# The opening of a two-layer decoder step written in a fixed order: first weights split behind the third turned block, high products ahead of block 4, rstd rows spread in one go

## The chip, the cores and the metric

The kernel runs on one core of a Trainium2 chip. A core has five engines that each work through a queue of their own in order: TensorE (PE in the profile; PEld are its weight loads), VectorE (DVE), ScalarE (ACT), GpSimd (POOL) and SyncE (SP, which here only issues DMA transfers). They wait for one another on semaphores. The metric is the time of one execution in microseconds (us), the median of several runs.

## What is computed

One step of a two-layer trunk, for 512 prompt tokens and 64 sample tokens (8 sequences of 8), model width 1024, all in 32-bit floats. Layer 0 begins with an RMSNorm and one input projection into 2560 columns, which the change is about; causal gating, differential attention over the prompt and over 64 pages of cached keys and values, an output projection and a SwiGLU follow, then a layer with a diagonal state-space scan and another SwiGLU.

```python
def rmsnorm(x, g):
    xf = x.astype(jnp.float32)
    y = xf * lax.rsqrt(jnp.mean(xf * xf, axis=-1, keepdims=True) + EPS)
    return (y * g.astype(jnp.float32)).astype(x.dtype)

def even_project(h, w_in, sgu_norm):      # h = rmsnorm(x, norm_mix[0])
    b, t, _ = h.shape
    p = h @ w_in
    uv = jax.nn.gelu(p[..., :2 * A_WIDTH])
    u = uv[..., :A_WIDTH]
    v = rmsnorm(uv[..., A_WIDTH:], sgu_norm)
    ...
    return u, v, q, k, vb
```

## The kernel before

The 576 tokens lie along the free dimension and the model width along the partitions, in 8 blocks of 128 (`k` from 0 to 7). x arrives token by token in rows, so each block is first turned by TensorE: four transposes of 128 x 128 into a PSUM tile `xT`, and a short one of the 64 sample tokens into `xU` (lines 430 to 450). x is loaded in two halves of columns, `load_x(0)` for blocks 0 to 3 and `load_x(1)` for blocks 4 to 7, five tiles `xt` each, with the first weights between them.

Every product of two f32 matrices is made of three at the faster rate of rounded operands: each operand is split into a high part (`gxh`, `wh`, rounded by a copy on ACT) and a low part (`gxl`, `wl`, the difference), and high x high, low x high and high x low are summed in PSUM. So a turned block is used three times: ACT scales it by the norm's weight into `gxh`, DVE makes `gxl`, and DVE copies the unscaled block to `x`, which SP stores to `dX` for the residual. Meanwhile the squares of x are summed along the width (`square`, on ACT with an accumulator, and two of the ten on POOL with a reduction on DVE).

The weights come in pairs of column blocks, 1 MB a load (`raw`, two buffers). A unit is one block of 128 output columns: `wsplit` makes `wh` and `wl` (two buffers each), and `unit_mm` runs 8 blocks x 3 products x 2 halves of 288 tokens, 48 matmuls. Ten pairs make twenty units. The first unit takes the blocks in order as they come (`kmajor`): for each block, the three products of the one half and then of the other. Its weight split is issued behind block 3 (`KSPL`), with the low part on POOL (`GLO`), that of the second unit on DVE.

The norm's factor per token, rstd, is applied late: `ev_scaled` multiplies a finished unit by `rb`, rstd spread over all partitions. `Stat0.steps` makes rstd out of the sums by a chain of small DVE operations (`rstd_from`, three Newton steps), and `bcast_rows` spreads it by five small matmuls into two PSUM tiles `rbp` and `rbq`; behind the second of them ACT may already copy the first 256 columns.

PSUM has eight banks: four for products (`mbank`, which also takes every second `xT`), four for all else (`bank`). SBUF blocks come from a ring of 44.

What sets the order: this is written in a language whose scheduler places each instruction on its engine's queue by its own forecast, apart from instructions wrapped in `keep`, which stay in program order, and stretches under `tc.manual_schedule()`, which are issued as written. The opening before uses `keep` for the turns; products, squares on POOL, weight splits and the DMAs of SP are placed by the scheduler. Behind the opening, side jobs (`tables`, which loads small constants, the mixer's weights `sgw` and the page table `ptt`; then `sample_attn`, which gathers pages `pg` through `pidx`, made of `ptt`, and turns each key page, `ktp`) are stepped in between units by `drv`.

## Time and profile before

| | us |
|---|---|
| runs shown (3) | 1392.58, 1394.92, 1396.45; median 1394.92 |
| the profiled execution | 1402.85 |
| its span, first to last instruction | 1401.1 |
| PE busy in the span | 1364.9 (97%) |
| DVE, ACT, POOL busy | 844.3, 484.8, 263.7 |
| first product (`acc`) of the projection | starts at 17.87 |
| third unit | starts at 36.05 |
| first page turned (`ktp`) | starts at 54.22 |

All later times are from the profiled execution, counted from the start of its span. A row of the timeline gives the start, the time until the instruction's end, the engine, the line, the operation, what it writes and reads, shapes, and how many alike were merged; in brackets stands how long the engine had been idle and who released it. Ends overlap the next start where work is pipelined, so the spacing of starts tells the rate. Engines other than the one that ends last may idle at no cost.

### The profile page before, as it was taken

Reading aid. Unit: us, or ns where it says so; the run is one execution under the profiler, and the core shown is the slowest. Engines: PE = TensorE matmul, PEld = TensorE weight load, DVE = VectorE, ACT = ScalarE, POOL = GpSimd, SP = SyncE. Lnnn points to the kernel's source line nnn. Section 1 sums busy time; section 2 is a strip of 40 time slices with the busy share of each in tenths; the row PEclk is TensorE's granted clock in tenths of the full one; section 3 lists DMA queues with packets and bytes.
Section 4 is the critical chain, followed back from the end, with each engine's and each line's share of the span. In section 5 each row is a group of like instructions: output and inputs, shape, how many; then the busy total and the mean of one; then the engine's idle time right before and its main releaser. Section 6 shows DMA issues by size and latency. Waiting matters only on the chain.

```text
span 1401.1 us, 27629 instructions
## 1 busy us (share of the span) xinstructions
PE 1364.9 (97%) x11382; PEld 1304.8 (93%) x11382; DVE 844.3 (60%) x1985; ACT 484.8 (35%) x875; POOL 263.7 (19%) x387
## 2 busy tenths in 40 slices
PE   8999999999999999999999989999999999999997
PEld 6888888879999999999999989999999999999997
DVE  5544667578699536887974697444343434443455
ACT  4234664434332223333322556233221221222234
POOL 2453543660000100444461000000000000000002
PEclk9999999999999999999999999999999999999999
DMA  8565544763333432554566791232323223313321
GB/s 248 167 202 178 173 146 127 220 192 93 89 87 114 121 91 73 161 154 135 142 191 216 205 284 57 68 91 61 91 69 111 63 75 106 89 56 98 91 61 69
DMA packets 192726, 177.38 MB, mean 127 GB/s; under 512 B 19420, under 2 KB 168280, under 8 KB 192600
## 3 DMA queue, kind: packets, MB, share of 16 engines
q1 hardware_dynamic: 172168, 118.18, 28.5%
q0 software_dynamic: 18912, 54.42, 13.3%
q10 hardware_dynamic: 1520, 3.02, 0.6%
q8 instruction: 90, 1.47, 0.4%
q14 instruction: 36, 0.29, 0.1%
HBM read 154.24 MB, written 25.53 MB: 128 GB/s over the span
## 4 chain that ended last, share of the span: by engine, by line
PE 84%; DVE 9%; DMA 2%; issue 2%; ACT 2%; SPq 1%; POOL 0%; ACTq 0%; POOLq 0%; DVEq 0%
PE acc L293 71%; PE ktp L808 2%; PE so L875 1%; PE ssc L789 1%; DVE wl L263 1%; PE S L652 1%; PE yp L1729 1%; PE yp L1723 1%; DMA xt<-in_x_sample_dram 1%; DVE x L1066 1%; PE O L685 1%; PE gT L1463 1%; PE satp L849 1%; PE vp L1666 0%; PE AT L677 0%
## 5 line engine op out<-in xcount | busy, mean ns | idle before, releaser
L293 PE MATMUL acc<-hi,wh 128*128 128x288 f32 x2400 | 713.6, 297 | 1.2 <-ACT hi L227 1.2
L293 PE MATMUL acc<-lo,wh 128*128 128x288 f32 x2400 | 707.3, 295 | 0.8 <-DVE lo L228 0.8
L293 PE MATMUL acc<-hi,wl 128*128 128x288 f32 x2400 | 707.5, 295 | 0.4 <-DVE wl L263 0.4
L293 PEld LDWEIGHTS acc<-hi,wh 128*128 128x128 f32 x2400 | 450.2, 188 | 8.3 <-issue 6.2
L293 PEld LDWEIGHTS acc<-lo,wh 128*128 128x128 f32 x2400 | 450.4, 188 | 1.3 <-DVE lo L228 1.3
L293 PEld LDWEIGHTS acc<-hi,wl 128*128 128x128 f32 x2400 | 450.5, 188 | 0.6 <-DVE wl L263 0.6
L260 ACT CAST wh<-raw 128x1024 fp32r<-128x1024 f32 (+2 forms) x194 | 182.8, 944 | 582.6 <-PE acc L293 416.3
L263 DVE TENSOR_TENSOR wl<-raw,wh 128x1024 fp32r<-128x1024 f32 (+2 forms) x193 | 211.7, 1097 | 58.5 <-ACT wh L260 56.7
L1139 DVE TENSOR_TENSOR tu<-acc,rb 128x288 f32<-128x288 f32 x88 | 40.3, 458 | 126.3 <-PE acc L293 126.0
L1876 POOL TENSOR_TENSOR sq<-sq,sq 128x288 f32<-128x288 f32 x12 | 9.6, 801 | 533.4 <-ACT sq L1872 533.4
L293 PE MATMUL acc<-gxh,wh 128*128 128x288 f32 x320 | 99.6, 314 | 0.9 <-DVE proj L390 0.9
L293 PE MATMUL acc<-gxh,wl 128*128 128x288 f32 x320 | 95.5, 301 | 0.6 <-DVE wl L263 0.6
L293 PE MATMUL acc<-gxl,wh 128*128 128x288 f32 x320 | 95.7, 300 | 0.0
L1129 DVE TENSOR_TENSOR tg<-acc,rb 128x288 f32<-128x288 f32 x88 | 39.9, 456 | 90.0 <-PE acc L293 89.0
L1149 DVE TENSOR_TENSOR x<-acc,x 128x288 f32<-128x288 f32 x96 | 43.3, 455 | 70.6 <-PE acc L293 70.5
L751 POOL DMA_INDIRECT pg<-in_cache_k_dram,pidx x64 | 65.5, 1023 | 84.1 <-PE ktp L808 48.8
L751 POOL DMA_INDIRECT pg<-in_cache_v_dram,pidx x64 | 66.0, 1031 | 63.8 <-PE so L875 37.8
L293 PEld LDWEIGHTS acc<-gxh,wh 128*128 128x128 f32 x320 | 60.8, 191 | 6.7 <-issue 6.0
L293 PEld LDWEIGHTS acc<-gxh,wl 128*128 128x128 f32 x320 | 60.7, 190 | 2.2 <-issue 1.1
L293 PEld LDWEIGHTS acc<-gxl,wh 128*128 128x128 f32 x320 | 61.1, 191 | 0.3 <-issue 0.2
L1516 POOL DMA_DIRECT2D dF<-Fn x32 | 20.0, 629 | 130.0 <-DVE Fn L1437 130.0
L227 ACT CAST hi<-tu 128x576 fp32r<-128x576 f32 x44 | 29.7, 676 | 35.0 <-DVE tu L1141 35.0
(464 smaller groups left out, 1601.2 us busy)
## 6 DMA issues: line engine op xcount, KB each, us to landing
raw<-in_w_ffn_in_dram SPq DMA_DIRECT2D x88, 512.0 KB
raw<-in_w_ffn_out_dram SPq DMA_DIRECT2D x24, 768.0 KB
raw<-in_w_in_even_dram SPq DMA_DIRECT2D x10, 1024.0 KB
raw<-in_w_glu_dram SPq DMA_DIRECT2D x16, 512.0 KB
raw<-in_w_out_even_dram SPq DMA_DIRECT2D x8, 512.0 KB
dF<-Fn POOLq DMA_DIRECT2D x32, 128.0 KB
dG<-gt POOLq DMA_DIRECT2D x16, 256.0 KB
dL<-dZ POOLq DMA_DIRECT2D x64, 64.0 KB
```

The costliest lines, as they stand in the source:

```text
L227: A.copy(hi, src)
L260: c = A.copy(hi[:, 0:nk], src)
L263: c = (lo_eng or V).tensor_tensor(lo[:, 0:nk], src, f32(hi[:, 0:nk]), op=ALU.subtract)
L293: PE.matmul(pts[hf], lhsT=w[:, k, :], rhs=x[:, c0:c1], start=(k == 0 and wi == 0), stop=(k == nk - 1 and wi == 2))
L652: PE.matmul(sp[:, 0:n], lhsT=qT[h][64 * e:64 * e + 64, P * i:P * i + P], rhs=kT[h][64 * e:64 * e + 64, 0:n], start=True, stop=True)
L685: PE.matmul(op[:, 0:P], lhsT=at[:, P * j:P * j + P], rhs=Vh[h][:, j, :], start=(j == 0), stop=(j == i))
L751: G.indirect_dma_start(out=t, out_offset=None, in_=src, in_offset=bass.IndirectOffsetOnAxis(ap=pidx[:, 8 * b + j:8 * b + j + 1], axis=0))
L808: PE.transpose(tp[:, P * h:P * h + P], pgt[:, P * h:P * h + P], ident)
L1129: V.tensor_tensor(half(t, hf), pt, half(stat.need(), hf), op=ALU.mult)
L1139: V.tensor_tensor(half(t, hf), pt, half(stat.need(), hf), op=ALU.mult)
L1149: V.tensor_tensor(half(nxt[m], hf), pt, half(cur[m], hf), op=ALU.add)
L1516: G.dma_start(out=dF[k][hh, :, c].rearrange("p (g n) -> p g n", g=4), in_=f[64 * c:64 * c + 64, :, 1:9, :].rearrange("p g d c -> p g (d c)"))
```

## The change

The opening, up to the second unit's end, is written out by hand under `manual_schedule`. Its parts are: (1) dummy matmuls on constants (`warm`: eight ahead of the first transpose, two ahead of each of the next three) into a PSUM tile that nobody reads; (2) blocks 0 to 3 turned in a row, the first unit's weights split behind block 2's evacuation on ACT, the low part on POOL; (3) the first two units go by `unit_ab`, which parts the products with the high weights (`a`, four a block) from those with the low weights (`b`, two a block); the `a` of blocks 0 to 2 stand ahead of block 4's turn, and the others are woven in between the turns; (4) all ten squares on ACT, five early and five behind the second unit's weight cast, whose low part moves from DVE to POOL; block 4's copy moves from DVE to ACT; (5) the rstd rows in one go, ahead of the second unit's last seven `b`, with the copy of the first 256 columns behind all five matmuls; (6) the third unit's low part on DVE ahead of the rows.

```diff
--- before.py
+++ after.py
@@ -33,7 +33,6 @@
 ULAG = 3
 MS = 6
 CUTS = ((0, 4), (4, 8))
-KSPL = 3
 NPIN = 4
 GLO = frozenset((0,))
 SP0, SP1, SP2, SP3 = 0.85, 1.0, 1.0, 1.0
@@ -207,15 +206,17 @@
         V.scalar_tensor_tensor(r, t, 1.5, y, op0=ALU.add, op1=ALU.mult)
         return r
 
-    def bcast_rows(rstd):
+    def bcast_rows(rstd, early=True):
         pb = [bank("rbp"), bank("rbq")]
         rb = rp.tile([P, NT], F32, tag="rb", name=nm("rb"))
         for i in range(5):
             n = P if i < 4 else 64
             c = P * (i % 4)
             PE.matmul(pb[i // 4][:, c:c + n], lhsT=rstd[0:n, i:i + 1].to_broadcast([n, P]), rhs=ident[0:n, 0:n], start=True, stop=True)
-            if i == 1:
+            if i == 1 and early:
                 A.copy(rb[:, 0:256], pb[0][:, 0:256])
+        if not early:
+            A.copy(rb[:, 0:256], pb[0][:, 0:256])
         V.tensor_copy(rb[:, 256:512], pb[0][:, 256:512])
         A.copy(rb[:, 512:NT], pb[1][:, 0:64])
         return rb
@@ -413,57 +414,70 @@
     V.memset(ssq0, 0.0)
     sqs = [(i, hf) for hf in range(2) for i in range(5)]
 
-    def square(E):
-        if not sqs:
-            return
-        i, hf = sqs.pop(0)
-        n = P if i < 4 else 64
-        x, acc = xt[i][hf][0:n], ssq0[0:n, 2 * i + hf:2 * i + hf + 1]
-        junk = blk("junk", (P, 512))
-        if E is A:
-            keep(A.activation(junk[0:n], x, AF.Square, accum_out=acc))
-        else:
-            G.tensor_tensor(junk[0:n], x, x, op=ALU.mult)
-            later.append((junk, n, acc))
-
-    later = []
-    for k in range(KD):
+    gx[:] = [(blk("gxh", dt=F32R), blk("gxl", dt=F32R)) for _ in range(KD)]
+    x0 = [None] * KD
+    turned0 = {}
+    parts = (slice(0, NP), slice(NP, NT))
+
+    def squares(n):
+        for _ in range(n):
+            i, hf = sqs.pop(0)
+            m = P if i < 4 else 64
+            A.activation(blk("junk", (P, 512))[0:m], xt[i][hf][0:m], AF.Square, accum_out=ssq0[0:m, 2 * i + hf:2 * i + hf + 1])
+
+    def warm(n):
+
+        w = bank("warm")
+        for i in range(n):
+            PE.matmul(w[:, 0:P], lhsT=ident, rhs=ones, start=True, stop=True)
+
+    def turn(k):
         hf, c = k // 4, (k % 4) * P
-        pa, pb = (bank("xT") if k % 2 else mbank("xT")), bank("xU")
+        pa, pb = (mbank("xT") if k in (0, 2) else bank("xT")), bank("xU")
         for i in range(4):
-            keep(PE.transpose(pa[:, P * i:P * i + P], xt[i][hf][:, c:c + P], ident))
-        keep(PE.transpose(pb[:, 0:64], xt[4][hf][0:64, c:c + P], ident[0:64, 0:64]))
-        hi = blk("gxh", dt=F32R)
-        lo = blk("gxl", dt=F32R)
-        x0 = blk("x")
-        gk = g_mix0[:, k:k + 1]
-        for pt, cs in ((pa, slice(0, NP)), (pb[:, 0:64], slice(NP, NT))):
-            keep(A.activation(hi[:, cs], pt, AF.Copy, scale=gk))
-            keep(V.scalar_tensor_tensor(lo[:, cs], pt, gk, f32(hi[:, cs]), op0=ALU.mult, op1=ALU.subtract))
-            keep(V.tensor_copy(x0[:, cs], pt))
-        SP.dma_start(out=dX[k], in_=x0)
-        gx[k] = (hi, lo)
-        square(A)
-        if k >= 5:
-            square(G)
-        if k == KSPL:
-            W.splits()
-    while sqs:
-        square(A)
+            if k == 0:
+                warm(8 if i == 0 else 2)
+            PE.transpose(pa[:, P * i:P * i + P], xt[i][hf][:, c:c + P], ident)
+        PE.transpose(pb[:, 0:64], xt[4][hf][0:64, c:c + P], ident[0:64, 0:64])
+        turned0[k] = (pa, pb[:, 0:64])
+        for pt, cs in zip(turned0[k], parts):
+            A.activation(gx[k][0][:, cs], pt, AF.Copy, scale=g_mix0[:, k:k + 1])
+
+    def rest(k):
+        for pt, cs in zip(turned0[k], parts):
+            V.scalar_tensor_tensor(gx[k][1][:, cs], pt, g_mix0[:, k:k + 1], f32(gx[k][0][:, cs]), op0=ALU.mult, op1=ALU.subtract)
+
+    def keep_x(k, E=None):
+        x0[k] = blk("x")
+        for pt, cs in zip(turned0.pop(k), parts):
+            (E or V.tensor_copy)(x0[k][:, cs], pt)
+        SP.dma_start(out=dX[k], in_=x0[k])
+
+    def unit_ab(u):
+
+        pts = [mbank("acc")[:, 0:HF] for _ in range(2)]
+
+        def mm(k, lows, first, last):
+            hi, lo = u["hl"]
+            xh, xl = gx[k]
+            for hf in range(2):
+                c = slice(HF * hf, HF * hf + HF)
+                ws = ((lo, xh),) if lows else ((hi, xh), (hi, xl))
+                for n, (w, x) in enumerate(ws):
+                    PE.matmul(pts[hf], lhsT=w[:, k, :], rhs=x[:, c], start=(first and n == 0), stop=(last and n == len(ws) - 1))
+        return pts, (lambda k: mm(k, False, k == 0, False)), (lambda k, last=False: mm(k, True, False, last))
 
     class Stat0:
         rb = None
 
         def steps(self):
             yield
-            for junk, n, acc in later:
-                V.tensor_reduce(acc, junk[0:n], axis=AX.X, op=ALU.add)
             s5 = small("s5", 5)
             V.tensor_reduce(s5, ssq0.rearrange("p (i h) -> p i h", h=2), axis=AX.X, op=ALU.add)
             r = rstd_from(s5, 5, DM)
             yield
             yield
-            self.rb = bcast_rows(r)
+            self.rb = bcast_rows(r, False)
 
         def start(self):
             self.gen = drv.add(self.steps(), 1.0)
@@ -474,7 +488,63 @@
             return self.rb
 
     st0 = Stat0()
-    st0.start()
+    with tc.manual_schedule():
+        A.activation(epst[:, 1:2], epst[:, 0:1], AF.Square)
+        squares(3)
+        u0, u1, u2 = W.q[0:3]
+        for k in range(4):
+            turn(k)
+            rest(k)
+            keep_x(k)
+            if k == 2:
+                u0["hl"] = wsplit(u0["ld"]["raw"], KD, 0, G)
+        squares(2)
+        p0, a0, b0 = unit_ab(u0)
+        for k in range(3):
+            a0(k)
+        turn(4)
+        rest(4)
+        turn(5)
+        keep_x(4, A.copy)
+        rest(5)
+        keep_x(5)
+        a0(3)
+        b0(0)
+        turn(6)
+        rest(6)
+        b0(1)
+        a0(4)
+        turn(7)
+        rest(7)
+        keep_x(6)
+        keep_x(7)
+        u1["hl"] = wsplit(u1["ld"]["raw"], KD, P, G)
+        squares(5)
+        b0(2)
+        b0(3)
+        b0(4)
+        for k in range(5, KD):
+            a0(k)
+            b0(k, k == KD - 1)
+        p1, a1, b1 = unit_ab(u1)
+        g0 = st0.steps()
+        next(g0)
+        next(g0)
+        for k in range(KD):
+            a1(k)
+        next(g0)
+        W.done = 1
+        W.loads()
+        u2["hl"] = wsplit(u2["ld"]["raw"], KD, 0)
+        b1(0)
+        next(g0, None)
+        for hf in range(2):
+            u0["evac"](hf, p0[hf])
+        for k in range(1, KD):
+            b1(k, k == KD - 1)
+        for hf in range(2):
+            u1["evac"](hf, p1[hf])
+        W.done, W.nsp = 2, 3
 
     def rows_out(srcT, h, po, smp):
         tp = bank("rows")
@@ -1079,7 +1149,6 @@
     def side(gen, pace):
         return drv.add(gen, pace)
 
-    W.run(1)
     tab = side(tables(), 1.0)
     W.run(4)
     drv.until(tab)
```

Three places show how the queues of the engines change. First PE, around the first product; `xT_266` and `xU_267` are block 6 and `gxh_149` block 0 before.

```order
L434 MATMUL xT_266<-ident,xt_117 128x128
L435 MATMUL xU_267<-ident,xt_119 128x64
L293 MATMUL acc_317<-gxh_149,wh_218 128x288
L293 MATMUL acc_317<-gxl_150,wh_218 128x288
L293 MATMUL acc_321<-gxh_149,wh_218 128x288
L293 MATMUL acc_321<-gxl_150,wh_218 128x288
L293 MATMUL acc_317<-gxh_149,wl_219 128x288
```

The same place in the change; `xT_234` is block 3, `gxh_142` block 0, `gxh_146` block 2 and `xT_267` block 4.

```order
L440 MATMUL xT_234<-ident,xt_103 128x128
L441 MATMUL xU_235<-ident,xt_105 128x64
L467 MATMUL acc_253<-gxh_142,wh_230 128x288
L467 MATMUL acc_253<-gxl_143,wh_230 128x288
L467 MATMUL acc_254<-gxh_142,wh_230 128x288
...
L467 MATMUL acc_254<-gxh_146,wh_230 128x288
L467 MATMUL acc_254<-gxl_147,wh_230 128x288
L440 MATMUL xT_267<-ident,xt_111 128x128
```

The first product stood behind seven turned blocks; it now stands behind four, and twelve products precede block 4's turn.

Second ACT, at the end of the opening, before: the last high parts alternate with squares, and the copies of the rows (`rb`) follow.

```order
L441 ACTIVATE gxh_273<-xU_267,gmix 128x64
L424 ACTIVATE junk_283,ssq_16_140<-xt_115 128x512
L441 ACTIVATE gxh_294<-xT_287,gmix 128x512
L441 ACTIVATE gxh_294<-xU_288,gmix 128x64
L424 ACTIVATE junk_304,ssq_16_140<-xt_119 64x512
L218 COPY rb_393<-rbp_391 128x256
```

The same place in the change, from block 7's high part on.

```order
L444 ACTIVATE gxh_156<-xU_321,gmix 128x64
L261 CAST wh_339<-raw_109 128x1024
L426 ACTIVATE junk_343,ssq_16_140<-xt_111 128x512
L426 ACTIVATE junk_345,ssq_16_140<-xt_113 128x512
L426 ACTIVATE junk_347,ssq_16_140<-xt_115 128x512
L426 ACTIVATE junk_349,ssq_16_140<-xt_117 128x512
L426 ACTIVATE junk_351,ssq_16_140<-xt_119 64x512
L261 CAST wh_435<-raw_121 128x1024
L219 COPY rb_443<-rbp_441 128x256
```

The cast of the second unit's weights and five squares now stand between the last high part and the rows.

Third SP, around the third load of weights, before (`dX_132` is the store of block 3, `sb_b`, `lamt`, `sgw`, `ptt` are the tables).

```order
L444 DMA dX_132<-x_208 128x576
L245 DMA raw_405<-in_w_in_even_dram 128x8x256
L444 DMA dX_133<-x_235 128x576
L444 DMA dX_134<-x_254 128x576
L444 DMA dX_135<-x_275 128x576
L444 DMA dX_136<-x_296 128x576
L536 DMA sb_b_430<-in_sgu_b_dram 128x512
```

The same in the change.

```order
L454 DMA dX_134<-x_293 128x576
L454 DMA dX_135<-x_331 128x576
L454 DMA dX_136<-x_335 128x576
L246 DMA raw_433<-in_w_in_even_dram 128x8x256
L606 DMA sb_b_507<-in_sgu_b_dram 128x512
L610 DMA lamt_510<-in_lambda_q_dram 128x64
```

The load moved from behind the fourth store to behind the eighth, directly ahead of the tables. Behind the first 235 rows or so of PE, and the first hundred of DVE, the two programs' orders are the same.

## The prediction

> **What bounds the kernel now.** I read the page's head and chain first, then the waits of PE (TensorE), then the opening in order of time.
>
> ```profile
> span 1401.1 us, 27629 instructions
> PEclk9999999999999999999999999999999999999999
> PE 84%; DVE 9%; DMA 2%; issue 2%; ACT 2%; SPq 1%; POOL 0%; ACTq 0%; POOLq 0%; DVEq 0%
> ...
> 10.00:20.00 10.00, 9.01 (x34) 6.15 (x33) 9.36 (x20) 9.74 (x26) 5.28 (x3) 1.00 1.04 338
> ...
> 60.00:100.00 40.00, 39.20 (x429) 34.94 (x429) 16.99 (x30) 12.64 (x19) 21.42 (x22) 1.00 0.64 188
> ```
>
> The end is PE's: 84% of the chain. The last two rows are stretches (length, then busy time of PE, weight loads, DVE, ACT, POOL, clock, DMA share, GB/s): PE is busy 9.01 of 10 us in the middle of the opening and 39.20 of 40 behind it. So what the opening saves on PE should arrive at the end unchanged, as long as nothing with a fixed time stands behind it. The new order of PE rows differs from the old only in the first 235 or so, and in both orders 216 products of the projection (`acc`) stand ahead of the first transpose of a key page (`ktp`). That point, at 54.22 us below, is my ruler.
>
> ```profile
> 2.62 0.26 PE L150 MATMUL vps<-ident,vstage 16*128 16x16 f32 x1 [2.62 <-DMA vstage<-in_norm_mix_dram]
> ...
> 8.27 1.11 PE L434 MATMUL xT<-ident,xt 128*128 128x128 f32 x4
> ...
> 9.62 1.11 PE L434 MATMUL xT<-ident,xt 128*128 128x128 f32 x4
> ...
> 18.52 0.44 PE L293 MATMUL acc<-gxh,wh 128*128 128x288 f32 x1
> 18.76 0.44 PE L293 MATMUL acc<-gxl,wh 128*128 128x288 f32 x1
> ...
> 22.86 0.29 PE L293 MATMUL acc<-gxl,wh 128*128 128x288 f32 x1
> 22.99 0.29 PE L293 MATMUL acc<-gxh,wl 128*128 128x288 f32 x1
> ...
> 23.66 0.60 PE L434 MATMUL xT<-ident,xt 128*128 128x128 f32 x4
> ...
> 54.22 1.03 PE L808 MATMUL ktp<-ident,pg 128*128 128x128 f32 x8
> ```
>
> A product costs 0.24 us from start to start at 18.5 us and 0.13 at 22.9. A turned block costs 1.34 us early (8.27 to 9.62; 0.262 a transpose), about 0.66 later (0.133 a transpose). The array runs at half rate until about 22.1 us, although the page's line of the granted clock reads nine tenths or more from the first slice on. Back-to-back transposes from 8.27 to 13 us did not end that; some 4.2 us of products from 17.87 on did.
>
> **The change, step by step** (times in the profiled execution).
>
> *Dummies and block 0.* A dummy is one f32 matmul, two records on PE (the row-spreading rows below show x2 for one). Eight stand behind `vps`, from 2.88 us: 16 records, 4.2 us at the slow 0.262, 2.1 at 0.133. Then come four transposes with six dummies between them and the short transpose, 17 records, 4.5 us or 2.3. All slow, block 0 is turned at 11.6 us; all fast, at 8.2, held by the rows of x. If the rate rises 4.2 us into the dummies, as it did into the products, it is 9.5, which I take: 1.2 us later than now, where block 1 starts at 8.27.
>
> ```profile
> 7.85 0.69 ACT L441 ACTIVATE gxh<-xT,gmix 128x512 fp32r<-128x512 f32 x1 [3.40 <-PE xT L434]
> 8.44 0.31 ACT L441 ACTIVATE gxh<-xU,gmix 128x64 fp32r<-128x64 f32 x1
> 8.63 0.63 ACT L424 ACTIVATE junk<-xt 128x512 f32<-128x512 f32 x1
> 9.43 0.69 ACT L441 ACTIVATE gxh<-xT,gmix 128x512 fp32r<-128x512 f32 x1
> 8.57 0.75 DVE L442 SCALAR_TENSOR_TENSOR gxl<-xT,gmix,gxh 128x512 fp32r<-128x512 f32 x1 [4.71 <-ACT gxh L441]
> 10.16 0.74 DVE L442 SCALAR_TENSOR_TENSOR gxl<-xT,gmix,gxh 128x512 fp32r<-128x512 f32 x1
> 13.57 2.01 ACT L260 CAST wh<-raw 128x1024 fp32r<-128x1024 f32 x2
> 14.72 2.36 POOL L263 TENSOR_TENSOR wl<-raw,wh 128x1024 fp32r<-128x1024 f32 x1 [11.50 <-ACT wh L260]
> ```
>
> *The ladder of blocks.* By these starts a high part costs ACT 0.78 us, a square 0.80, a weight cast 0.95 to 1.0; a block costs DVE 1.6. From 9.5: DVE starts at 10.3 and frees blocks 0 to 3 at 11.9, 13.5, 15.1 and 16.7. The pool has four banks, so block 3's short turn waits for block 1 to be freed at 13.5, and the first product starts at 13.6 (17.87 now). Twelve products and block 4's turn last to 15.9; block 5's turn waits for block 3's bank (16.7) and ends at 17.4. ACT copies block 4 until 19.05, which frees the bank for block 6 (turned 19.65); block 7 is turned at 21.1 and its high part done at 22.0. Then ACT casts the second unit's weights (22.95) and squares five tiles, 4.0 us, until 27.0. The weights of the first unit are needed at 11.9; they may land as late as 13.57, where their cast ran without a wait: 0.3 us more. POOL's low part, 2.36 us, ends at 15.4 and 25.5, each before PE asks for it.
>
> ```profile
> 26.61 0.15 DVE L462 TENSOR_REDUCE s<-ssq 128x5 f32<-128x10 f32 x1
> 29.02 0.17 DVE L180 SCALAR_TENSOR_TENSOR rsy<-rst,rsy 128x5 f32<-128x5 f32 x1
> ...
> 32.84 0.60 PE L216 MATMUL rbp<-ident,rsy 128*128 128x128 f32 x4
> 33.37 0.43 PE L216 MATMUL rbq<-ident,rsy 64*128 64x64 f32 x2
> 34.99 0.42 DVE L219 COPY rb<-rbp 128x256 f32<-128x256 f32 x1 [0.90 <-ACT wh L260]
> 35.45 0.82 DVE L390 TENSOR_TENSOR proj<-acc,rb 128x288 f32<-128x288 f32 x2
> 36.05 0.37 PE L293 MATMUL acc<-gxh,wh 128*128 128x288 f32 x1 [0.91 <-DVE proj L390]
> 37.46 0.40 PE L293 MATMUL acc<-gxh,wl 128*128 128x288 f32 x1 [0.60 <-DVE wl L263]
> ```
>
> *Rows of rstd, and the third unit.* The chain of small DVE operations takes 2.6 us (26.61 to 29.19), so rstd is there at 29.7. PE has run out of ready products at 28.8 and waits 1 us. The rows in one go are ten records, 1.3 us, to 31.1; Fourteen products are left, 1.85 us, to 32.95. Beside them ACT and DVE copy the rows out (0.42 on DVE) and DVE evacuates the first unit (0.82 for both halves). The two stalls of today (0.91 on the evacuation, 0.60 on `wl`) go: the low part stands ahead of the rows on DVE, and the copies and the first evacuation end at 32.2, so that a bank is free when PE comes. From there to the ruler are 120 products, 15.9 us, and 1.3 us of other PE work (constants, mixer weights, block diagonal): 50.15 instead of 54.22. **4.1 us saved, if the rate stays fast from 7 us on.** Now the first product comes at 17.87, and the 36.35 us to the ruler are 28.6 us of products, 2 us lost to the slow rate, 1.5 of stalls and some 4 of turns, rows and small work.
>
> *Does it stay fast?* The trace has one place that tells.
>
> ```profile
> 288.23 0.29 PE L293 MATMUL acc<-hi,wl 128*128 128x288 f32 x1
> 290.73 0.66 PE L907 MATMUL soT<-ident,OS 128*128 128x128 f32 x4 [2.20 <-DVE S L654]
> ...
> 291.93 0.44 PE L293 MATMUL acc<-lo,wh 128*128 128x288 f32 x1
> 292.17 0.44 PE L293 MATMUL acc<-hi,wl 128*128 128x288 f32 x1
> ...
> 295.51 0.30 PE L293 MATMUL acc<-lo,wh 128*128 128x288 f32 x1
> 295.65 0.29 PE L293 MATMUL acc<-hi,wl 128*128 128x288 f32 x1
> ```
>
> After an idle 2.20 us the spacing is 0.24 again from about 291.9 to 295.3, 3.4 us. In the new order PE has only 16 short transposes and two waits between 9.5 and 13.6 us, 2.1 us of 4.1, and later waits of 0.85 and 0.8 us at blocks 5 and 6. I take the rate to fall once and stay low for one or two such stretches. In 3.4 us at 0.24 PE does 1.5 us less work; some 0.6 of that hides in the waits for banks, so 0.9 each. I subtract 1.5: **2.6 us saved.** The ends are nothing subtracted, 4.1, and slow until the dense stretch, rival 2.
>
> [...]
>
> **Rivals.** *1. The rate stays fast.* For it: eight transposes between products, at 54.22, ran at 0.13 each, and the products before and behind them too. Against it: the thin 4.1 us. Saved 4.1: 1390.8. With dummies that are fast at once and block 0 at 8.2, 1.3 us more: 1389.5.
>
> *2. The dummies only delay.* All slow to 24 us, block 0 is turned at 11.6, each block costs 1.34, and the sum puts the third unit at 37.6: ruler 54.8, 0.6 us later than now: 1395.5. Repeated falls land between this and the forecast.
>
> *3. The tables land late; slower.*
>
> ```profile
> 18.52 0.40 SPq L245 DMA_DIRECT2D raw<-in_w_in_even_dram  x1
> 27.09 0.66 SPq L536 DMA_DIRECT2D sb_b<-in_sgu_b_dram  x1
> 29.79 0.43 SPq L542 DMA_DIRECT2D sgw<-in_sgu_w_dram  x1
> 30.26 5.18 DMA ptt<-in_page_table_dram
> ```
>
> The third weight load moves on SP from behind four stores of x, at 18.52, to behind all eight and POOL's second low part, 25.5; the tables queue right behind it, `sgw` at 28.7, `ptt` at 29.2. `ptt` took 5.2 us; a megabyte ahead of it adds 3 (338 GB/s in the stretch from 10 to 20 us): 37.4. PE wants `sgw` 40 products into the third unit, at about 40, and the gathers behind `ptt` have some 14 us to the ruler. Each us past 40 is a us lost; past 42.6 the saving is gone, and 0.3% slower needs 47, 18 us after issue. Price at 47: 1399.1.
>
> **How the numbers follow.** The profiled execution took 1402.85 us against a span of 1401.1 and a median of 1394.92; a saving in the opening is the same in both, so I subtract it from the median: 1394.92 - 2.6 = **1392.3**. What a measurement can tell from no change is about 0.3%, 4.2 us. Chances: forecast (saved 1.2 to 4.1) 0.5; rival 1 and all beyond 4.1 0.24; rival 2 (saved -1.5 to 1.2) 0.19; rival 3 0.07. Rival 1 reaches 4.2 where block 0 also comes early, or where the timed runs scatter, as the three shown do by 4 us; I give faster its whole 0.24, slower 0.07, within 0.69. The range runs from rival 1's 1389.5, less 1 for that scatter, to rival 2's 1395.5 and 0.5: 1388.5 to 1396.
>
> **What would show it.** Block 0 turned near 9.5 us; the first product near 13.6; the last square near 27 and rows at 30 to 31; the third unit at 33 to 35.5; `ktp` at 50 to 52.5; a spacing of 0.24 somewhere between 12 and 22 us. It is wrong if the spacing is 0.13 throughout, if PE waits for `sgw` or a page, or if waits behind the ruler take the gain back.

## The result, and the profile after

| | before | the change |
|---|---|---|
| median of 8 runs | 1397.12 us | 1388.06 us |
| range of these runs | 1392.58 to 1401.12 | 1387.67 to 1389.14 |
| the profiled execution, its span | 1402.85, 1401.1 | 1389.14, 1387.4 |
| PE busy | 1364.9 | 1360.6 |
| first product, third unit, first turned page | 17.87, 36.05, 54.22 | 13.67, 32.52, 50.33 |

The ratio is 0.9936, with a 95% interval from 0.9922 to 0.9951: faster by more than a measurement's 0.3%. The time lies 0.4 us below the predicted range. The forecast was subtracted from the median of the first three runs of before, 1394.92; that of all eight is 1397.12, so the change saves 6.9 us by the one and 9.06 by the other. The page's head, clock and chain of the change:

```profile
span 1387.4 us, 27686 instructions
PEclk9999999999999999999999999999999999999999
PE 85%; DVE 8%; DMA 3%; issue 2%; ACT 1%; POOL 1%; SPq 0%; POOLq 0%; ACTq 0%; DVEq 0%
```

The same two stretches of the change as were shown of before:

```profile
10.00:20.00 10.00, 8.20 (x50) 6.08 (x51) 9.01 (x22) 7.81 (x20) 2.39 (x1) 1.00 0.94 300
60.00:100.00 40.00, 40.00 (x446) 35.75 (x439) 16.95 (x30) 12.72 (x20) 23.41 (x23) 1.00 0.68 207
```

PE is the end as before. In the middle of the opening it is busy for less time (8.20 us against 9.01) and starts half as many instructions again (50 against 34): each is shorter. Behind the opening it is busy for 40.00 of 40 us, where it was 39.20. The opening of the change in order of time, PE and the rows of the other engines on which the prediction's steps rest:

```profile
9.95 0.24 PE L441 MATMUL xU<-ident,xt 64*128 64x64 f32 x1 [0.60 <-DMA xt<-in_x_sample_dram]
...
13.37 0.24 PE L441 MATMUL xU<-ident,xt 64*128 64x64 f32 x1 [0.88 <-DVE x L453]
13.67 0.40 PE L467 MATMUL acc<-gxh,wh 128*128 128x288 f32 x1
13.91 0.30 PE L467 MATMUL acc<-gxl,wh 128*128 128x288 f32 x1
14.04 0.30 PE L467 MATMUL acc<-gxh,wh 128*128 128x288 f32 x1
...
28.83 1.23 DVE L264 TENSOR_TENSOR wl<-raw,wh 128x1024 fp32r<-128x1024 f32 x1
29.23 1.05 PE L215 MATMUL rbp<-ident,rsy 128*128 128x128 f32 x8
31.18 0.82 DVE L391 TENSOR_TENSOR proj<-acc,rb 128x288 f32<-128x288 f32 x2
32.52 0.30 PE L294 MATMUL acc<-gxh,wh 128*128 128x288 f32 x1
...
50.33 1.03 PE L878 MATMUL ktp<-ident,pg 128*128 128x128 f32 x8
```

The spacing behind the first product is 0.24 us, as it is behind others that follow turns (17.71 to 17.95), and from then on 0.13: no stretch of 0.24. The third unit starts without a wait, 0.4 us ahead of the sum for an array that stays fast (32.95), and the first turned page comes at 50.33 (50.15 in that sum): 3.89 us earlier than before. But the two executions differ by 13.7 us at the end. The other 9.8 us open up between 54 and 345 us, where the orders of the two programs are the same. Of PE's waits there, the seven longest kinds before, and all kinds after (us in all, times, longest):

```profile
PE soT L907 <- DVE S L654: 2.2, 1, 2.2
PE satp L849 <- DVE src L843: 1.2, 1, 1.2
PE AT L677 <- ACT p L660: 1.1, 1, 1.1
PE oTp L702 <- DVE o L697: 0.9, 1, 0.9
PE ssn L826 <- issue: 0.8, 2, 0.4
PE rowt L484 <- ACT S L794: 0.7, 1, 0.7
PE satn L857 <- ACT p L660: 0.6, 1, 0.6
```

```profile
PE so L945 <- DMA pg<-in_cache_v_dram,pidx: 1.3, 2, 0.7
PE AT L747 <- ACT p L730: 1.0, 1, 1.0
PE so L945 <- issue: 0.3, 1, 0.3
PE oTp L772 <- DVE o L767: 0.2, 1, 0.2
```

One of the waits that are gone, `rowt` on ACT's copy `S`, followed back: the last scores of a bank (`ssc`), the maximum over them, the copy, the transpose that takes the bank. Before:

```profile
66.33 0.64 PE L789 MATMUL ssc<-kt,Qz 128*32 128x128 f32 x16
67.88 0.69 DVE L792 TENSOR_REDUCE mx<-ssc 128x1 f32<-128x512 f32 x1 [1.93 <-PE ktp L808]
68.61 0.58 ACT L794 COPY S<-ssc 128x512 f32<-128x512 f32 x1 [3.20 <-issue]
69.25 0.30 PE L484 MATMUL rowt<-ident,proj 128*64 128x128 f32 x1 [0.68 <-ACT S L794]
```

And in the change:

```profile
62.45 0.64 PE L859 MATMUL ssc<-kt,Qz 128*32 128x128 f32 x16
63.16 0.69 DVE L862 TENSOR_REDUCE mx<-ssc 128x1 f32<-128x512 f32 x1 [1.09 <-PE ssc L859]
64.52 0.30 PE L554 MATMUL rowt<-ident,proj 128*64 128x128 f32 x1
```

The scores end at 66.97 and DVE is idle, yet the maximum starts at 67.88, 0.91 us later; in the change it starts 0.07 us after them. I call this a late start: an instruction of DVE or ACT that starts over 0.3 us after both the matmul that it waits for has ended in the records and its own engine is free. (Some lie near 0.3 us, or wait for more than one matmul, so a count can differ by two to four with the way of reading.) Between 60 and 303 us the execution of before has 26 (17 on DVE, 9 on ACT), all behind matmuls; the change has none. Whether they go with the change was the first question.

### The profile page after: what moved, and what is told of

Its sections match the earlier page's. It is cut to its first block, busy times and chain, and to the rows that moved or that the text cites. A ratio compares the mean times of both kernels' runs of the same rounds, so it can differ in the third digit from the quotient of the medians.

```text
span 1387.4 us, 27686 instructions
## 1 busy us (share of the span) xinstructions
PE 1360.6 (98%) x11410; PEld 1304.8 (94%) x11410; DVE 840.2 (61%) x1980; ACT 488.2 (35%) x882; POOL 263.5 (19%) x386
## 3 DMA queue, kind: packets, MB, share of 16 engines
q0 software_dynamic: 18912, 54.42, 13.3%
## 4 chain that ended last, share of the span: by engine, by line
PE 85%; DVE 8%; DMA 3%; issue 2%; ACT 1%; POOL 1%; SPq 0%; POOLq 0%; ACTq 0%; DVEq 0%
PE acc L294 72%; PE ktp L878 2%; PE ssc L859 1%; PE so L945 1%; DVE wl L264 1%; PE S L722 1%; PE yp L1798 1%; DMA pg<-in_cache_v_dram,pidx 1%; PE O L755 1%; DMA sgw<-in_sgu_w_dram 1%; DMA raw<-in_w_in_even_dram 1%; PE yp L1792 1%; DVE x L1136 1%; PE satp L919 1%; PE gT L1532 1%
## 5 line engine op out<-in xcount | busy, mean ns | idle before, releaser
L294 PE MATMUL acc<-gxh,wh 128*128 128x288 f32 x288 | 90.2, 313 | 0.0
L294 PE MATMUL acc<-gxh,wl 128*128 128x288 f32 x288 | 85.9, 298 | 0.0
L294 PE MATMUL acc<-gxl,wh 128*128 128x288 f32 x288 | 85.6, 297 | 0.0
L294 PEld LDWEIGHTS acc<-gxh,wh 128*128 128x128 f32 x288 | 54.3, 188 | 4.9 <-issue 4.2
L294 PEld LDWEIGHTS acc<-gxh,wl 128*128 128x128 f32 x288 | 54.1, 188 | 1.2 <-issue 1.1
L294 PEld LDWEIGHTS acc<-gxl,wh 128*128 128x128 f32 x288 | 54.3, 189 | 0.3 <-issue 0.2
```

The source lines that it names most:

```text
L294: PE.matmul(pts[hf], lhsT=w[:, k, :], rhs=x[:, c0:c1], start=(k == 0 and wi == 0), stop=(k == nk - 1 and wi == 2))
```

## The experiments

All times of marks below come from each run's one profiled execution. "Late" counts late starts; "at half" lists the stretches up to 400 us in which the granted clock reads 0.50, by start and length; the ratio is to the kernel before in the same session (runs made together on one chip), with its interval.

| run | first product | first turned page | late | at half | median us (runs) | ratio |
|---|---|---|---|---|---|---|
| before, as profiled first | 17.87 | 54.22 | 26 | 291.9: 3.4 | | |
| the change, result | 13.67 | 50.33 | 0 | none | 1388.06 (8) | 0.9936 |
| e1 before again | 19.49 | 56.43 | 25 | 38.8: 3.4 | 1404.69 (1) | |
| e2 no dummies | 13.19 | 51.10 | 25 | 353.2: 3.4 | 1400.70 (12) | 0.9973 (0.9957 to 0.9989) |
| e3 23 dummies | 16.27 | 52.34 | 27 | 287.3: 3.4 | 1404.11 (12) | 0.9992 (0.9975 to 1.0008) |
| e4 before, with dummies | 19.12 | 54.78 | 24 | 15.2: 6.8; 291.7: 3.4; 356.5: 6.8 | 1405.10 (12) | 0.9997 (0.9982 to 1.0013) |
| e5 change again | 13.01 | 49.26 | 0 | 341.9: 6.8 | 1391.68 (11) | 0.9965 (0.9951 to 0.9978) |
| e6 10 dummies | 13.63 | 49.73 | 0 | none | 1391.35 (12) | 0.9962 (0.9948 to 0.9976) |
| e7 before, paired | 19.11 | 55.19 | 26 | 289.2: 3.4; 357.4: 3.4 | 1403.50 (1) | |
| e8 change, paired | 13.35 | 49.88 | 23 | 351.0: 3.4 | 1398.85 (1) | |
| e9 turns first | 20.63 | 54.21 | 23 | 12.6: 10.2; 289.1: 3.4; 354.0: 6.8 | 1403.45 (12) | 0.9982 (0.9968 to 0.9997) |
| e10 rows late | 13.16 | 52.10 | 22 | 13.4: 3.4; 286.5: 3.4; 354.7: 3.4 | 1400.34 (12) | 0.9966 (0.9947 to 0.9985) |
| e11 wide sums | 13.25 | 49.33 | 25 | 192.4: 6.8; 288.0: 3.4 | 1397.38 (6) | 0.9946 (0.9928 to 0.9964) |
| e12 change beside e11 | 12.49 | 49.54 | 24 | 13.3: 3.4; 286.3: 3.4; 351.2: 6.8 | 1399.04 (6) | 0.9958 (0.9943 to 0.9974) |

The sessions are e1 to e4, e5 and e6, e7 to e10, e11 and e12.

**Are the late starts the change's doing, and what are the dummies worth? (e1 to e4)**

e1 is the kernel before, unchanged.

> The kernel before, unchanged, profiled a second time. In its first profile 17 DVE and 9 ACT instructions between 60 and 302 us start 0.3 to 1.8 us later than the matmul that they wait for ends and their own engine is free; in the profile of the change none does. If this comes with the old order (theory A) or with the old moment of the page stage (B) or with the array being slow at the start (C), the second profile has some 15 to 25 such late starts again, spread over the same stretch, and the time is 1395 to 1402 us. If it was chance in one execution (D), there are few or none, the first turned page still starts at 54.2 us, and the time is about 1388.1 + 3.9 = 1392.

e2 takes the dummies out of the change, e3 adds 15:

```diff
-            if k == 0:
-                warm(8 if i == 0 else 2)
```

```diff
-                warm(8 if i == 0 else 2)
+                warm(23 if i == 0 else 2)
```

> The change without its 14 dummy matmuls, all else as in the change. All theories: the spacing is 0.24 us until the array has been dense for some 4 us, so blocks 0 to 3 are turned at 1.34 us each and the first products are slow; the first turned page comes 1 to 2.5 us later than in the change, 51.3 to 52.8 us. Theory A (the gain behind the opening comes from the order) and B (from the moment): no late starts on DVE and ACT behind 60 us, 1389 to 1391 us. Theory C (from the array being fast early): late starts as in the kernel before, 1394 to 1397 us.

> The change with 23 dummies instead of 8 ahead of the first transpose, 15 more: at 0.27 us each some 4 us, so that the first turned page starts at 54.2 us or a little later, as before the change, while the array is fast as early and every order is that of the change. Theory A and C: no late starts behind 60 us, 1388.1 + 4 = 1392. Theory B (the page stage suffers when it begins at that moment, against loads and gathers that do not move with it): late starts come back, 1396 to 1398 us.

e4 puts them into the kernel before; every other row keeps its place.

```diff
+            if k == 0:
+                w = bank("warm")
+                for _ in range(8 if i == 0 else 2):
+                    keep(PE.matmul(w[:, 0:P], lhsT=ident, rhs=ones, start=True, stop=True))
             keep(PE.transpose(pa[:, P * i:P * i + P], xt[i][hf][:, c:c + P], ident))
```

> The kernel before with the same 14 dummies ahead of its first transposes, all other rows in their old order. All theories: the array is fast from about 7 us, the products from 17.9 us on run at 0.13 and the first turned page comes 1 to 2.5 us earlier than before, 51.7 to 53.2 us. Theory A: late starts stay, 1394 to 1396 us. Theory C: late starts go, 1388 to 1391 us. Theory B: in between, since the moment lies in between.

All four have the late starts, for the most part at the same program points and of like sizes (the maximum above: 0.91, 0.90, 0.94 and 0.91 us), in the old order and in the new, with the array fast early or not, and with the first turned page anywhere from 51.1 to 56.4 us. So A, B and C fall alike, and chance in one execution does too. What was left was the change with exactly its own dummies, or the session.

On the opening they told more. Without dummies the first turned page comes at 51.10, 0.8 to 1.8 us after that of the change in its five profiles (49.26 to 50.33). Fifteen more do not cost 4 us but 2.0 to 3.1, probably since part of them lies in time in which block 0 otherwise waits for x (0.60 us at its last row in the result). And in the old order the dummies are worth nothing that can be measured:

```profile
8.00:15.00 7.00, 4.81 (x28) 3.20 (x27) 5.02 (x13) 5.74 (x17) 0.00 (x0) 1.00 1.08 332
15.20:22.00 6.80, 6.30 (x24) 5.02 (x25) 6.34 (x11) 5.75 (x14) 6.05 (x7) 0.50 0.87 284
```

These are two stretches of e4 (length, busy time and instructions of PE, weight loads, DVE, ACT and POOL, then granted clock, DMA share, GB/s). PE is thin from 8 to 15 us (28 instructions, 4.81 of 7 us), and then the clock reads 0.50 for 6.8 us, to 22.0, where the old order became fast without any dummies (22.1). This is the fall that the forecast had put into the change. The twelve runs of e4 have a mean granted clock of 0.988, the 29 of before in that session 0.992.

**The change or the session? (e5 to e8)**

> The change, unchanged, run again beside the kernel before on one chip. In the four runs so far the late starts of DVE and ACT behind 58 us stand at the same program points with the same sizes whatever the opening (0.9 us at the maximum over the first scores, 1.2 at the first masked scores), with and without dummies, in the old order and in the new. Theory A' (the change as a whole, with exactly its dummies, is free of them): no late starts, 1388 us, a ratio to before below 0.990. Theory D' (they belong to the chip or the session, not to the kernel; the profiles of before and after were not taken under the same conditions): late starts at the same points, some 1399 us, and a ratio to before near 0.996, which is the opening's 4 to 5.5 us alone.

e6 is the change with `warm(10 if i == 0 else 2)`.

> The change with 10 dummies instead of 8 ahead of the first transpose, two more (0.53 us of PE, partly in a wait for the rows of x). The opening should end within 0.5 us of the change's. Theory A' says that such a small step from the change's own count may already bring the late starts back; theory D' says that this kernel and the change do the same: late starts in both or in neither, and times within 1 us of one another.

Neither has a late start, but the ratio was 0.9965: the opening's gain, not 9 us. So the kernel before was profiled beside the change:

> The kernel before, unchanged, profiled on the same chip as the next run. Two chips have been met: on one every kernel showed the late starts of DVE and ACT behind 58 us, on the other two openings showed none. Theory D' (late starts belong to the chip): this run and the next have them both or have neither. Theory E (the old opening has them on every chip, the new one on the first chip only): this run has them and the next does not, and the lead of the change grows from 4 us at the first turned page to some 9 us at 310 us.

> The change, unchanged, beside the run above. Theory D': the lead over the run above is 4 to 7 us at the first turned page, as the opening makes it, and the same within 1.7 us (half a stretch of 3.4 us at half rate, each of which is seen in the granted clock) at every later mark up to 310 us. Theory E: the lead grows by 4 us or more between them without any difference in the granted clock.

Both have the late starts. The place shown above, in the paired change:

```profile
62.01 0.64 PE L859 MATMUL ssc<-kt,Qz 128*32 128x128 f32 x16
63.53 0.69 DVE L862 TENSOR_REDUCE mx<-ssc 128x1 f32<-128x512 f32 x1 [1.91 <-PE ktp L878]
64.90 0.30 PE L554 MATMUL rowt<-ident,proj 128*64 128x128 f32 x1 [0.66 <-ACT S L864]
```

It is the same program as the one whose maximum started at 63.16, 0.07 us after its scores; here it starts 0.88 us after them. Theory D' holds: in each of the four sessions all kernels profiled have the late starts or none has. (The last session was on the chip of e5 and e6 and had them, so it isn't the chip as such.) Two marks of the pair, before first:

```profile
55.19 1.03 PE L808 MATMUL ktp<-ident,pg 128*128 128x128 f32 x8
...
289.75 1.11 PE L907 MATMUL soT<-ident,OS 128*128 128x128 f32 x4 [2.10 <-DVE S L654]
```

```profile
49.88 1.03 PE L878 MATMUL ktp<-ident,pg 128*128 128x128 f32 x8
...
284.06 0.66 PE L977 MATMUL soT<-ident,OS 128*128 128x128 f32 x4 [2.10 <-DVE nmx L728]
```

The lead is 5.31 us at the first turned page and 5.69 at `soT`, 234 us of program later, and 4.65 at the end, where the two profiles have fallen to half rate at different places. What the opening saves arrives, apart from such stretches. The late starts cost the change 6.6 us between these two marks (234.18 us here; in the result's profile `soT` came at 277.92, 227.59 after its first page). The first profile of before, 1402.85, was from such a session, that of the change was not: their 9.8 us behind the opening compare two sessions, not two kernels. From the first turned page to the end it takes 1346.9 us in the first profile of before, 1346.6 in e7 and 1347.2 in e8, which is the change; without late starts 1337.1 in the result, 1336.4 in e6 and 1342.2 in e5, whose clock fell more often.

**Which part of the opening? (e9, e10)**

e9 puts the first twelve products back behind the turns of blocks 4 to 6, on PE alone; the six that stood ahead of block 6's turn come behind it too, to keep their order:

```diff
         p0, a0, b0 = unit_ab(u0)
-        for k in range(3):
-            a0(k)
         turn(4)
...
-        a0(3)
-        b0(0)
         turn(6)
         rest(6)
+        for k in range(4):
+            a0(k)
+        b0(0)
         b0(1)
```

> The change with one thing undone: the twelve products with the high weights of blocks 0 to 2 stand behind the turns of blocks 4 to 6 again, on PE alone; dummies, rows and all other engines as in the change. If the forward products carry the gain, as the ladder of blocks has it: the first product at 17.5 to 19 us instead of 13 to 13.7, the last block turned about 1 us earlier than in the change, and since the twelve products (1.6 us) no longer fill PE's waits for the banks, the third unit and the first turned page come 1 to 2 us later than in the change. Rival: ACT's squares and the rstd chain set the rows' moment, so these products have slack: rows and first turned page stay within 0.5 us of the change's.

The granted clock is the third column from the end; first e9, then e8 from the same session, in which the products stand in front:

```profile
12.60:22.80 10.20, 7.07 (x24) 4.88 (x25) 6.32 (x16) 6.21 (x15) 2.35 (x1) 0.50 0.90 301
```

```profile
12.60:22.80 10.20, 8.72 (x56) 7.22 (x57) 8.11 (x21) 7.64 (x18) 2.40 (x1) 1.00 0.94 299
```

The loss is 4.3 us at the first turned page, over twice what was expected: the products do more than fill waits. With them in front the clock reads 1.00 over these 10.2 us (e8), without them 0.50 (e9). In e9 PE waits for banks (1.16 us at block 6) and x (1.10, 0.35, 0.27 and 0.22 at block 4), the first product comes at 20.63 (17.5 to 19 was expected), the clock falls at 12.6 us for three stretches, and nearly all that the opening had gained is gone (54.21, against 49.88 in e8 and 55.19 in e7). That is not this one profile's chance: the mean granted clock of e9's twelve runs is 0.988, that of e10's twelve and of the 23 of before in the same session 0.991.

e10 undoes parts 5 and 6, the rows and the third low part:

```diff
-        u2["hl"] = wsplit(u2["ld"]["raw"], KD, 0)
-        b1(0)
+        for k in range(KD):
+            b1(k, k == KD - 1)
         next(g0, None)
         for hf in range(2):
             u0["evac"](hf, p0[hf])
-        for k in range(1, KD):
-            b1(k, k == KD - 1)
+        u2["hl"] = wsplit(u2["ld"]["raw"], KD, 0)
```

> The change with parts 5 and 6 undone: the rows of rstd stand behind all of the second unit's products, the first unit's evacuation behind them and the third unit's low part behind that; first four blocks, dummies and products as in the change. If the two stalls of before (0.91 us on the evacuation, 0.60 on the third low part) come from this order, PE waits for the copies and the evacuation (0.8 to 1.6 us) and for the low part (0.5 to 1.2 us) at the third unit, and the first turned page comes 1.5 to 2.8 us later than in the change. Rival: the rows would come only when the chain of small operations is done anyway, so little is lost: less than 0.7 us.

```profile
34.02 0.39 PE L294 MATMUL acc<-gxh,wh 128*128 128x288 f32 x1 [1.21 <-ACT wh L261]
35.43 0.40 PE L294 MATMUL acc<-gxh,wl 128*128 128x288 f32 x1 [0.60 <-DVE wl L264]
```

Two stalls are back at the third unit, 1.21 and 0.60 us. The first ends with the third unit's cast on ACT, which goes back behind the rows' copies with this edit, and not with the first unit's evacuation as before (0.91); rows, cast and low part are undone together here and are not told apart. The first turned page is 2.2 us later than in e8. The rows come 2.26 us later (31.35 and 29.09), 1.86 of it the fourteen products now ahead of them; the other 0.4 I put down to the stretch at half rate from 13.4 us. Behind the rows the stalls take as long as the fourteen products did.

**What makes the runs scatter? (e11, e12)**

In most profiles, eight of thirteen at each place, the clock falls for one or two stretches near 342 to 357 and 953 to 971 us. Just there the sums of squares of two norms go over PE: 22 records with one column of ones. In e5:

```profile
339.80:341.90 2.10, 2.10 (x19) 1.99 (x18) 1.29 (x2) 0.90 (x2) 0.00 (x0) 1.00 0.08 17
341.90:348.70 6.80, 6.80 (x30) 6.80 (x31) 2.00 (x12) 0.00 (x0) 0.00 (x0) 0.50 0.54 149
```

PE isn't idle there for a moment. e11 gives these products 64 columns of ones:

```diff
...
-                PE.matmul(self.pb[0:n, i:i + 1], lhsT=src[:, P * i:P * i + n], rhs=ones[:, 0:1],
+                PE.matmul(self.pb[0:n, 64 * i:64 * i + 64], lhsT=src[:, P * i:P * i + n], rhs=ones[:, 0:64],
...
```

> The change, and beside it the sums of squares of the two norms that go over TensorE (22 records near 342 and near 950 us) taken with 64 columns of ones in place of one column, so that each of these small products streams 64 columns where it streamed one; the sums themselves are the same. In the profiles so far the granted clock fell to half for one or two stretches of 3.41 us right behind these places in most executions (at 342 and 953 us in one, at 351 and 959 in another, at 357 in a third) and not at all in the profile of the change, and the starts of these stretches lie on a grid of 3.41 us that runs freely. Theory F: the scatter between executions is the phase of that grid against the thin stretches, in which the array is given one column at a time. Then no half-rate stretch stands within 10 us behind the two places, the mean granted clock is 0.994 to 0.995 in nearly all runs, and the median falls to about that of the change's fastest runs: 2 to 4 us below the change of the same call, with a smaller scatter. Rival: what counts is waits and transposes around them; the stretches stay, and the time is that of the change or 0.5 us more.

> The change, unchanged, on the chip of the run above, for comparison: by theory F it scatters over 4 to 6 us with the mean granted clock (0.991 to 0.995, some 1.4 us for each 0.001), and its fastest runs come within 1 us of the median of the run above. Against the kernel before a ratio near 0.996 to 0.997, as in the last pairs; if the 0.9936 of the first comparison was the rule, 0.994.

First e11 behind both places, then e12:

```profile
354.70:361.50 6.80, 6.80 (x53) 6.61 (x52) 4.12 (x16) 2.71 (x4) 0.00 (x0) 1.00 0.42 113
963.00:966.40 3.40, 3.40 (x28) 3.40 (x28) 2.01 (x12) 0.00 (x0) 0.00 (x0) 1.00 0.48 131
```

```profile
351.20:358.00 6.80, 6.80 (x30) 6.80 (x30) 2.00 (x12) 0.14 (x1) 0.00 (x0) 0.50 0.50 139
962.20:965.60 3.40, 3.40 (x15) 3.40 (x15) 2.00 (x12) 0.00 (x0) 0.00 (x0) 0.50 0.52 147
```

At neither place does e11 fall. Alone that shows little, since four profiles with narrow products (before, the result, e3, e6) have no fall at either place. The grid tells more. In each profile all stretches at half rate start a whole number of times 3.4133 us apart (a double stretch lasts 6.827): in the first profile of before at 291.92, 803.92 and 1394.42 us, 150 and 173 times; in the result at 790.17 and 1380.67, 173 times; in e5 two of them at 341.9 and 952.9, 179 times. So the edges of these intervals can be laid over the whole profile. In the thirteen profiles with narrow products the 22 records (2.60 us at the full rate) lie 26 times on such a grid. In the 16 cases where 1.98 us or more of them lay in one interval, the clock fell at that interval's end; in the ten with 1.84 us or less it did not fall. In e11 it was 2.71 us at the second place, more than in any of the 16, and the clock did not fall; at the first it was 1.97, between the two groups, which tells little.

Theory F holds for these places, as far as one profile with wide products can show it, but they are not the only ones: the clock of three of e11's six runs is 0.991 or 0.992, and its profile fell at 192.4 us. The runs scatter no less than those of e12 (5.4 and 4.9 us), where less was expected. The median is 1.7 us below that of e12, 6.9 below before; with six runs each and overlapping intervals it is not shown that this version beats the change.

## Why the prediction was wrong

Range and sign: 1392.3 was forecast, 1388.5 to 1396.0 the range, "faster" had 0.24. The time is 1388.06.

*Does it stay fast?* This is the step that failed: "I take the rate to fall once and stay low for one or two such stretches", and with it the 1.5 us subtracted. In the result the rate did not fall in the opening (the first fall is at 790.2 us). Such a fall was seen in the old order with dummies (e4, 6.8 us) and without the forward products (e9, 10.2 us). With the change's front, it came in two of seven profiles (e10 and e12, 3.4 us at 13.3). There it cost about 1 us: block 0 was turned 0.5 us earlier in e12 than in e5 (8.22 and 8.74), yet the rows came 0.45 later (28.75 and 28.30). So the likeliest case was rival 1, and 1.5 was a price for something that came in two profiles of seven.

What the step left out is where the grid lies. I had counted PE's work from 9.5 to 13.6 as one thin stretch. What went with a fall is the work in one whole interval of the 3.4133 us grid (see e11). Here are the two intervals around the thin stretch in e8, then in e12:

```profile
9.62:13.03 3.41, 2.48 (x15) 1.64 (x15) 3.17 (x9) 2.97 (x7) 0.00 (x0) 1.00 1.07 375
13.03:16.45 3.42, 2.76 (x17) 2.24 (x17) 3.23 (x9) 2.51 (x8) 2.40 (x1) 1.00 1.08 270
```

```profile
9.84:13.26 3.42, 1.83 (x12) 1.42 (x12) 3.42 (x10) 3.04 (x7) 0.95 (x1) 1.00 1.06 360
13.26:16.67 3.41, 3.41 (x16) 2.94 (x15) 2.20 (x6) 1.61 (x6) 1.44 (x1) 0.50 1.09 305
```

The clock falls behind e12's first interval and not behind e8's. Counted by the matmul records that start in an interval, up to 20 us (the view counts those still running at its start too, so 10 are x12 in e12): those before the falls have 7 (e4), 11 (e9), 10 (e12) and 12 (e10), and every other one at full rate, in e4, e9 and the seven profiles, has 13 or more. In the result an edge at 11.93 cuts the thin stretch: 17 records lie in the interval ahead of it and 16 in the one behind, twelve of them the forward products. Without these (e9) PE runs thin for some 11 us, in which more than one whole interval lies wherever the grid stands.

That a stretch of turns lets the rate fall was my estimate from before, where transposes from 8.27 to 13 us left the array slow. No run shows it for an array that is fast: in e8's interval (9.62 to 13.03) all 15 records are transposes and the clock stays at 1.00, while in e12's, which has 10 records and a fall behind it, products run from 12.49 on. Five of the seven profiles have no fall.

*The size of the opening's gain.* Rival 1's 4.1 us were met by the profiles that I compared (3.89). But my base was one execution, and a lucky one: the kernel before has its first turned page at 54.22, 55.19 and 56.43 us in three profiles, the change at 49.26 to 50.33 in five (e11's opening is the change's). Within a session the lead was 5.3 (e7 and e8). Part of it is when x lands (block 0's short transpose before at 7.98, 8.66 and 9.33), which I had priced at nothing, part a fall of the clock at 38.8 us in e1. So of the 4.2 us between the forecast and the time, 1.5 are the fall, some 1.2 the base (5.3 for 4.1), and the 1.5 that are left I put down to the scatter.

*What the opening saves arrives at the end unchanged.* Right: 5.31 and 5.69 us in the pair, 4.65 at its end. The growth of the lead in the two first profiles would have refuted it, had they been of one session.

*The scatter.* I allowed 1 us beyond the cases. Each 0.001 of the mean granted clock is about 1.4 us: in the session of e5 the five runs of before at 0.995 average 1393.1 and the four at 0.991 1398.6; the change has 1388.6 (two runs at 0.994) and 1392.9 (three at 0.991). The means of all runs there differ by 5.1 us and their clocks by 0.0005, so at equal clock the change leads by some 5.7 us. In the first comparison all eight runs of the change were at 0.994 or 0.995; the eight of before range over 8.5 us, 1392.6 to 1401.1. That is the range of before in the session of e5 (1392.0 to 1401.2), which had no late starts, and not of the others (1399.9 to 1410.7), so late starts do not explain the lead of 9.06. This lead is then 5 to 6 of the opening and the rest of stretches at half rate, which the runs of before would have had and those of the change had not. That split is argued, since the clocks of those runs of before weren't kept. Why all eight of the change escaped, when its later runs average 0.992, stays open. Later comparisons of the unchanged kernel gave 0.9965 and 0.9958.

*The rest of the ladder* held: block 0 at 9.95 (9.5 forecast, but by another way: the array became fast at 8.51, 5.7 us behind the first dummy where 4.2 was taken, and then block 0 waited 0.60 for x), first product 13.67 (13.6), the rows at 29.23 and the third unit at 32.52 (32.95), both stalls gone, and e10 brings stalls of 1.2 and 0.6 us back. *Rival 2* (the dummies only delay) is wrong for the change; in the old order (e4) its result came, no gain, but by a fall behind a fast start. *Rival 3* came only just into sight. In the result the transposes of `sgw` (`wps`) start at 38.47, released by its landing at 38.42:

```profile
38.47 0.42 PEld L635 LDWEIGHTS wps<-ident,sgw 128*128 128x128 f32 x4 [0.34 <-DMA sgw<-in_sgu_w_dram]
```

PE itself is idle there for 0.11 us, so the sign "PE waits for `sgw`" came, at a price near nothing. No page is waited for ahead of the first turned page.

## What to carry to other kernels

Work that was moved forward into a thin stretch of TensorE was worth more here than the waits that it filled, and with it the clock held: the change lost 4.3 us when its first products went back and the clock read 0.50 for 10.2 us (e9), while the same dummies gave nothing in the old order (e4, ratio 0.9997). What counted was not a thin stretch as such but how much of it fell into one interval of the 3.4133 us grid, whose place differed from run to run (edges at 11.93 us in the result, 9.62 in e8, 9.84 in e12): the short one, 4.1 us by the forecast, brought a fall in two of seven profiles, a chance to be priced; the long one, some 11 us in e9, brought one of 10.2 us, and the mean clock of e9's twelve runs is 0.988 where that of e10's is 0.991. Compare two profiles only if they were taken together: a lead that grows where the two programs are the same can be a sign of the session, as the 9.8 us behind the opening were, and one run of the old kernel beside the new one settles it. Before pricing a range, read the scatter of the mean granted clock over the runs; here each 0.001 of it was about 1.4 us.

## What the runs showed that was not expected

- Late starts: in three of four later sessions, and in the first profile of before, 22 to 27 instructions of DVE and ACT start 0.3 to 2.8 us after the recorded end of the matmul that they wait for, for the most part at the same program points, only while pages are gathered (56 to 303 us), in all kernels of the session. They cost 6.6 us. The semaphore updates kept in the traces show that it is TensorE's signal that is late: for the maximum shown, the scores end at 66.98, the update stands at 67.857 and the maximum starts at 67.881; in the change these are 63.09, 63.138 and 63.160. So DVE and ACT are prompt: in the first profile of before the late starts of DVE and five of those of ACT lie 0.022 to 0.025 us behind an update of TensorE. For the maximum shown, TensorE's next update follows at 67.917, 0.06 us behind the late one, though four transposes (0.53 us) lie between the two, so these two signals come bunched. What holds them up, and what sets the session's condition, is open.
- The clock falls to 0.50 for one or two stretches of 3.41 us although PE is never idle, behind 22 products of one column each (2.60 us), in all 16 cases in which 1.98 us or more of them lay in one interval of the 3.4133 us grid; with 64 columns, which take 0.27 us more (2.87), it did not fall with 2.71 us in one. No idle gap was needed: in e5 PE is busy for 2.10 of the 2.10 us ahead of the fall at 341.9.
- The half rate at the very start of these kernels isn't in the granted clock (it reads 1.00 while products are 0.24 us apart at 18.5 us before), the later falls are (0.50, and products 0.24 us apart, from 291.92 us in before). The trace's first entry of the clock stands where the array becomes fast: at 22.26 us before and at 8.51 in the change.
